# Evicting the up-projection's products ahead of the preceding tile's convolution

## The chip, the cores and the metric

One core of a Trainium2 chip runs the whole program. The metric is device time in microseconds (us) from start to end of one execution, lower is better. The engines that matter are TensorE (PE in the profile; its weight loads are PEld), VectorE (DVE), ScalarE (ACT), GpSimd (POOL) and SyncE (SP, which issues the DMAs).

## The reference, cut to what matters

The model is a trunk of two layers: a token mixer (gated DeltaNet, then mLSTM), each followed by a feed-forward block with a causal convolution of three taps. The change touches the first half of that block, `h @ w_up` and what is done with it:

```python
FFN_DIM = 2816; FFN_CONV = 3; D_MODEL = 1024          # 16 + 1024 tokens

def conv_ffn(h, w_up, conv_w, conv_b, w_down):
    u = causal_depthwise_conv(h @ w_up, conv_w) + conv_b
    gate, up = u[..., :FFN_DIM], u[..., FFN_DIM:]
    return (jax.nn.silu(gate) * up) @ w_down
```

## The kernel before

Features lie on partitions, tokens along the free axis; the 1040 tokens are cut into two halves `t` of 520, and each half into two quarters `n` of 260. The 5632 rows of `w_up` make 22 tiles `j`: 128 gate features (`h = 0`) and the 128 up features that go with them (`h = 1`). Every fp32 product is three matmuls of split operands (`mm3`, L229 to L231): high by high, high by low, low by high.

`ffn_plan` sets the order of the tiles in each layer. Tiles 0 to 5 are first done for half 0 alone, by plain products (`plain`). Then come, six times, a **pair** (tile 6 to 11, both halves) and a **single** (tile 0 to 5, half 1 alone), and then the pairs 12 to 21. Pairs and singles use Strassen's scheme: `quad` makes seven weight combinations from four loaded blocks, and a half needs seven products of four features blocks each, 12 matmuls of 260 columns. So a single has 7 products and a pair 14, the two halves alternating.

`combine` (L193) takes product `i` of a half out of its PSUM bank as soon as it is done. Product 0 is copied by ACT into the temporary `m1` (L199). Every later product is added by DVE (L196) to a temporary, into another temporary or into one of the four results `u`; product 3 takes two such adds. In the rows the names lose their digits: `m_u` is m1, `u_u` is u2 or u3, `u` a result. The products rotate through four PSUM banks (tags `pj` and `sp`, two each, L95 to L101): a product can start when the product four before it has been evicted.

After the last product of a tile its **convolution** follows: for each half, quarter and `h`, ACT scales `u` into a PSUM bank (`z`, L1272), DVE adds the two earlier taps (L1274, whose last step for `h = 1` writes `y`), ACT applies silu (L1276), POOL multiplies gate and up (L1277), and SP stores the result (L1279).

The weights of the tiles ahead are made in between: SP loads a block (L168), DVE forms the combinations (L171, L174, L175, L177: s1, s3, s2, s4), ACT rounds each to its high part (L137, `wh`), POOL subtracts for the low part (L138, `wl`). The combination s2 is written over a11 (L175, after a11's split), and s4 over s2 (L177, after s2's split). There are five slots for split weights, so the split of a weight waits until TensorE is done with the weight five before it.

Each engine works its instructions off in one order. It is set at build time by a scheduler that places an instruction, by priority, in the order of the program; `tc.high_priority(n)` moves what is inside it ahead by `n` of its steps. The accumulations of the down-projection had it before (in `second`); the evictions in `combine` did not. The three temporaries of a half (`temps`, L214) came from the ring `C` of 19 pages, which also holds the results `u` and the products `y`.

Of the kernel before, what the change touches and what calls it, by code (L numbers as in the profile page):

```python
# [29 lines left out]
QB = HB // 2  # L30
# [6 lines left out]
N_PAGES = 19  # L37
# [44 lines left out]
class Trunk:  # L82
# [111 lines left out]
    def combine(self, i, ps, tmp, out):  # L194

        add = lambda o, u: self.nc.vector.tensor_tensor(o, ps[:, :QB], u, ALU.add)  # L196
        m1, u2, u3 = tmp
        if i == 0:
            self.nc.scalar.copy(m1, ps[:, :QB])  # L199
        elif i == 1:  # L200
            add(u2, m1)
        elif i == 2:
            add(u3, u2)
        elif i == 3:
            add(out[3], u3)
            add(u2, u2)
        elif i == 4:
            add(out[1], u2)
        elif i == 5:
            add(out[2], u3)  # L210
        else:
            add(out[0], m1)

    def temps(self, name):  # L214
        return [self.page("C", f"{n}_{name}", N_PAGES)[:, :QB] for n in ("m1", "u2", "u3")]

    def queue_weights(self, sources, ahead):

# [1275 lines left out]
```

## Time and profile before

| | |
|---|---|
| three runs | 3479.31, 3480.08, 3485.89 us (median 3480.08) |
| the profiled execution | 3479.74 us, of which the span from first to last instruction is 3477.9 |
| busy share of the span | PE 92%, PEld 89%, DVE 68%, POOL 48%, ACT 46% |
| up-projection with pairs and singles, layer 1 | about 1458 to 1885 us from the span's start |
| the same, layer 2 | about 2771 to 3200 us |

The profile is of one execution. A row of a timeline gives the start, the duration, the instruction, and in brackets how long its engine was idle just before and what released it. Matmuls overlap in the pipeline: each is shown with some 0.28 us though one starts every 0.12 us, so the spacing of their starts is what counts. A row of busy time by stretch gives the stretch and its length, then the busy time and the number of instructions of PE, PEld, DVE, ACT and POOL, then the granted TensorE clock as a share of full speed, the DMA share and GB/s. A row of waits gives who waited for whom, the total in us, how often, and the longest.

### The profile page before, as it was taken

Reading aid. Unit: us, or ns where it says so; the run is one execution under the profiler, and the core shown is the slowest. Engines: PE = TensorE matmul, PEld = TensorE weight load, DVE = VectorE, ACT = ScalarE, POOL = GpSimd, SP = SyncE. Lnnn points to the kernel's source line nnn. Section 1 sums busy time; section 2 is a strip of 40 time slices with the busy share of each in tenths; the row PEclk is TensorE's granted clock in tenths of the full one; section 3 lists DMA queues with packets and bytes.
Section 4 is the critical chain, followed back from the end, with each engine's and each line's share of the span. In section 5 each row is a group of like instructions: output and inputs, shape, how many; then the busy total and the mean of one; then the engine's idle time right before and its main releaser. Section 6 shows DMA issues by size and latency. Waiting matters only on the chain. (4 is left out here: it accounts for less than half of the span.)

```text
span 3477.9 us, 68427 instructions
## 1 busy us (share of the span) xinstructions
PE 3208.6 (92%) x25368; PEld 3105.4 (89%) x25368; DVE 2368.7 (68%) x5143; ACT 1606.1 (46%) x3390; POOL 1653.5 (48%) x1890
## 2 busy tenths in 40 slices
PE   8999999999998997889999989899998898999998
PEld 6899988988998997888999989899998788999998
DVE  7777787777777559776666484534479766667474
ACT  5455554555545335644544343323355644445232
POOL 2434443443433444576665434323344577665453
PEclk9999999999999999999999999999999899999999
DMA  3010110101101344322223453211134422224452
GB/s 116 25 37 31 34 34 28 34 32 33 34 32 52 105 157 139 122 89 80 85 74 127 146 179 119 84 38 56 55 104 159 145 81 86 74 74 131 133 177 86
DMA packets 234510, 297.73 MB, mean 86 GB/s; under 512 B 20684, under 2 KB 167104, under 8 KB 234176
## 3 DMA queue, kind: packets, MB, share of 16 engines
q1 hardware_dynamic: 234176, 293.37, 26.0%
q8 instruction: 199, 3.26, 0.4%
q14 instruction: 135, 1.11, 0.1%
HBM read 240.06 MB, written 53.23 MB: 84 GB/s over the span
## 5 line engine op out<-in xcount | busy, mean ns | idle before, releaser
L229 PE MATMUL pj_gi<-xh_in,wh_gi 128*128 128x348 f32 x1152 | 393.7, 342 | 5.7 <-ACT wh_gi L137 3.8
L231 PE MATMUL pj_gi<-xh_in,wl_gi 128*128 128x348 f32 x1152 | 395.5, 343 | 0.9 <-POOL wl_gi L138 0.9
L230 PE MATMUL pj_gi<-xl_in,wh_gi 128*128 128x348 f32 x1152 | 392.9, 341 | 0.0
L229 PE MATMUL dn_f<-so_f,wh_f 128*128 128x260 f32 x1344 | 383.5, 285 | 8.1 <-ACT y L1276 3.9
L231 PE MATMUL dn_f<-so_f,wl_f 128*128 128x260 f32 x1344 | 380.5, 283 | 1.9 <-POOL wl_f L138 1.9
L230 PE MATMUL dn_f<-so_f,wh_f 128*128 128x260 f32 x1344 | 380.6, 283 | 0.0
L138 POOL TENSOR_TENSOR wl_f<-wr_f,wh_f 128x512 fp32r<-128x512 f32 x168 | 225.3, 1358 | 243.0 <-PE dn_f L230 102.7
L138 POOL TENSOR_TENSOR wl_u_s<-wr_u,wh_u_s 128x512 fp32r<-128x512 f32 x176 | 228.7, 1303 | 99.6 <-ACT wh_u_s L137 98.6
L1274 DVE SCALAR_TENSOR_TENSOR z<-u,fcw,z 128x260 f32<-128x260 f32 x528 | 244.3, 487 | 42.6 <-ACT z L1272 38.9
L229 PEld LDWEIGHTS dn_f<-so_f,wh_f 128*128 128x128 f32 x1344 | 254.0, 189 | 9.7 <-ACT y L1276 4.3
L437 DVE TENSOR_TENSOR acc_f<-acc_f,dn_f 128x260 f32<-128x260 f32 x320 | 132.7, 420 | 188.7 <-PE dn_f L231 187.6
L231 PEld LDWEIGHTS dn_f<-so_f,wl_f 128*128 128x128 f32 x1344 | 254.2, 189 | 2.4 <-POOL wl_f L138 2.3
L230 PEld LDWEIGHTS dn_f<-so_f,wh_f 128*128 128x128 f32 x1344 | 254.2, 189 | 0.2
L1272 ACT ACTIVATE z<-u,fcb,fcw 128x260 f32<-128x260 f32 x352 | 189.2, 566 | 138.0 <-DVE u L196 136.5
L229 PEld LDWEIGHTS pj_gi<-xh_in,wh_gi 128*128 128x128 f32 x1152 | 221.7, 192 | 8.0 <-ACT wh_gi L137 4.1
L231 PEld LDWEIGHTS pj_gi<-xh_in,wl_gi 128*128 128x128 f32 x1152 | 221.9, 193 | 2.3 <-POOL wl_gi L138 1.1
L230 PEld LDWEIGHTS pj_gi<-xl_in,wh_gi 128*128 128x128 f32 x1152 | 221.7, 192 | 0.7 <-issue 0.2
L138 POOL TENSOR_TENSOR wl_gi<-wr_gi,wh_gi 128x512 fp32r<-128x512 f32 x96 | 132.3, 1379 | 158.6 <-ACT wh_gi L137 152.0
L138 POOL TENSOR_TENSOR wl_u_a<-wr_u,wh_u_a 128x512 fp32r<-128x512 f32 x132 | 171.2, 1297 | 68.1 <-ACT wh_u_a L137 68.0
L693 DVE SCALAR_TENSOR_TENSOR gy<-u_g,c_gdn_conv_w_g,gy 128x348 f32<-128x348 f32 x288 | 188.2, 664 | 7.9 <-ACT gy L691 5.4
L137 ACT CAST wh_u_s<-wr_u 128x512 fp32r<-128x512 f32 x176 | 106.9, 614 | 183.1 <-PE up L230 149.7
L137 ACT CAST wh_f<-wr_f 128x512 fp32r<-128x512 f32 x168 | 103.0, 617 | 173.2 <-PE dn_f L230 119.4
(501 smaller groups left out, 11665.7 us busy)
## 6 DMA issues: line engine op xcount, KB each, us to landing
wr_u<-in_ffn_w_up_dram SPq DMA_DIRECT2D x224, 256.0 KB, 2.7
wr_f<-in_ffn_w_down_dram SPq DMA_DIRECT2D x176, 256.0 KB, 2.8
wr_gi<-in_gdn_w_in_dram SPq DMA_DIRECT2D x96, 256.0 KB, 2.6
h<-y SPq DMA_DIRECT2D x176, 130.0 KB, 2.4
si_f<-h SPq DMA_DIRECT2D x88, 260.0 KB, 3.5
wr_go<-in_gdn_w_out_dram SPq DMA_DIRECT2D x64, 256.0 KB, 2.7
wr_mi<-in_ml_w_in_dram SPq DMA_DIRECT2D x44, 256.0 KB, 2.6
o_g<-gy SPq DMA_DIRECT2D x48, 174.0 KB, 1.8
```

Of the source, the lines that this page charges most:

```text
L137: nc.scalar.copy(hi, part(raw))
L138: nc.gpsimd.tensor_tensor(lo, part(raw), hi.bitcast(F32), ALU.subtract)
L229: nc.tensor.matmul(out, w[0], x[0], start=start, stop=False)
L230: nc.tensor.matmul(out, w[0], x[1], start=False, stop=False)
L231: nc.tensor.matmul(out, w[1], x[0], start=False, stop=stop)
L437: nc.vector.tensor_tensor(acc[m][n], acc[m][n], ps, ALU.add)
L693: ins = nc.vector.scalar_tensor_tensor(y, u[:, j : j + BS], taps[:, j : j + 1], y, ALU.mult, ALU.add)
L1272: nc.scalar.activation(z, p[:, 2 : 2 + QB], AF.Identity, scale=taps[:, 2:3], bias=self.fcb[:, tt : tt + 1])
L1274: nc.vector.scalar_tensor_tensor(z if i or not h else y[h], p[:, i : i + QB], taps[:, i : i + 1], z, ALU.mult, ALU.add)
```

## The change

`combine` wraps its instructions in `high_priority(300)`, and the temporaries come from three other tags of two buffers each: m1 from `part`, u2 from `rs`, u3 from `sum`. Those tags exist already, for norms and sums outside this stretch. The arithmetic is the same.

```diff
--- before.py
+++ after.py
@@ -195,6 +195,10 @@
 
         add = lambda o, u: self.nc.vector.tensor_tensor(o, ps[:, :QB], u, ALU.add)
         m1, u2, u3 = tmp
+        with self.tc.high_priority(300):
+            self.combine_now(i, ps, add, m1, u2, u3, out)
+
+    def combine_now(self, i, ps, add, m1, u2, u3, out):
         if i == 0:
             self.nc.scalar.copy(m1, ps[:, :QB])
         elif i == 1:
@@ -212,7 +216,7 @@
             add(out[0], m1)
 
     def temps(self, name):
-        return [self.page("C", f"{n}_{name}", N_PAGES)[:, :QB] for n in ("m1", "u2", "u3")]
+        return [self.page(tag, f"{n}_{name}", 2)[:, :QB] for n, tag in (("m1", "part"), ("u2", "rs"), ("u3", "sum"))]
 
     def queue_weights(self, sources, ahead):
```

The order of the matmuls is the same but for four of them at the start of the down-projection. On DVE, ACT, POOL and SP the order changes only within the two up-projections. The lines after the new ones carry numbers higher by 4 (L199 is L203, L1272 is L1276, L1274 is L1278, L1276 is L1280).

First place, DVE: the end of pair 9's convolution while single 3's products are running. `u_u` and `u_3_..` are single 3's adds (`up_3_1_i` is its product `i`), `z_9` and `y_9` the convolution, and `wr_u_0_10` the weights of pair 10. Before:

```order
L1274 SCALAR_TENSOR_TENSOR z_9_1_0_1_21581<-u_9_1_0_1_21334,fcw_17463,z_9_1_0_1_21581 128x260
L1274 SCALAR_TENSOR_TENSOR y_9_1_1_0_21572<-u_9_1_1_0_21333,fcw_17463,z_9_1_1_0_21573 128x260
L1274 SCALAR_TENSOR_TENSOR z_9_1_0_1_21581<-u_9_1_0_1_21334,fcw_17463,z_9_1_0_1_21581 128x260
L1274 SCALAR_TENSOR_TENSOR z_9_1_1_1_21588<-u_9_1_1_1_21335,fcw_17463,z_9_1_1_1_21588 128x260
L175 TENSOR_TENSOR wr_u_0_10_0_21594<-wr_u_0_10_4_21598,wr_u_0_10_0_21594 128x512
L1274 SCALAR_TENSOR_TENSOR y_9_1_1_1_21587<-u_9_1_1_1_21335,fcw_17463,z_9_1_1_1_21588 128x260
L196 TENSOR_TENSOR u_u_3_1_21636<-up_3_1_1_21656,m_u_3_1_21635 128x260
L196 TENSOR_TENSOR u_u_3_1_21637<-up_3_1_2_21670,u_u_3_1_21636 128x260
L177 TENSOR_TENSOR wr_u_0_10_0_21594<-wr_u_0_10_3_21597,wr_u_0_10_0_21594 128x512
L196 TENSOR_TENSOR u_3_1_1_1_21641<-up_3_1_3_21684,u_u_3_1_21637 128x260
L196 TENSOR_TENSOR u_u_3_1_21636<-up_3_1_3_21684,u_u_3_1_21636 128x260
L196 TENSOR_TENSOR u_3_1_0_1_21640<-up_3_1_4_21699,u_u_3_1_21636 128x260
```

and with the change, where the add of product 1 stands three rows above the first row shown:

```order
L196 TENSOR_TENSOR u_u_3_1_21637<-up_3_1_2_21670,u_u_3_1_21636 128x260
L1278 SCALAR_TENSOR_TENSOR z_9_1_0_0_21566<-u_9_1_0_0_21332,fcw_17463,z_9_1_0_0_21566 128x260
L1278 SCALAR_TENSOR_TENSOR z_9_1_0_1_21581<-u_9_1_0_1_21334,fcw_17463,z_9_1_0_1_21581 128x260
L1278 SCALAR_TENSOR_TENSOR y_9_1_1_0_21572<-u_9_1_1_0_21333,fcw_17463,z_9_1_1_0_21573 128x260
L1278 SCALAR_TENSOR_TENSOR z_9_1_0_1_21581<-u_9_1_0_1_21334,fcw_17463,z_9_1_0_1_21581 128x260
L1278 SCALAR_TENSOR_TENSOR z_9_1_1_1_21588<-u_9_1_1_1_21335,fcw_17463,z_9_1_1_1_21588 128x260
L175 TENSOR_TENSOR wr_u_0_10_0_21594<-wr_u_0_10_4_21598,wr_u_0_10_0_21594 128x512
L1278 SCALAR_TENSOR_TENSOR y_9_1_1_1_21587<-u_9_1_1_1_21335,fcw_17463,z_9_1_1_1_21588 128x260
L196 TENSOR_TENSOR u_3_1_1_1_21641<-up_3_1_3_21684,u_u_3_1_21637 128x260
L196 TENSOR_TENSOR u_u_3_1_21636<-up_3_1_3_21684,u_u_3_1_21636 128x260
L177 TENSOR_TENSOR wr_u_0_10_0_21594<-wr_u_0_10_3_21597,wr_u_0_10_0_21594 128x512
L196 TENSOR_TENSOR u_3_1_0_1_21640<-up_3_1_4_21699,u_u_3_1_21636 128x260
```

The adds of products 1 and 2 move ahead of eight and six steps of the convolution and of L175, and the two adds of product 3 move ahead of s4 (L177); the adds of products 4, 5 and 6 stay behind L177.

Second place, ACT: the same stretch. `m_u_3` is the copy of single 3's product 0, `wh_u_1_3` the last two weights of single 3, and `wh_u_0_10` the first of pair 10. Before:

```order
L1276 ACTIVATE y_9_0_0_0_21535<-z_9_0_0_0_21536 128x260
L137 CAST wh_u_1_3_a_21314<-wr_u_1_3_2_21283 128x512
L1272 ACTIVATE z_9_1_0_0_21566<-u_9_1_0_0_21332,fcb_17464,fcw_17463 128x260
L1272 ACTIVATE z_9_1_1_0_21573<-u_9_1_1_0_21333,fcb_17464,fcw_17463 128x260
L137 CAST wh_u_1_3_a_21318<-wr_u_1_3_3_21284 128x512
L1276 ACTIVATE y_9_0_0_1_21550<-z_9_0_0_1_21551 128x260
L1272 ACTIVATE z_9_1_0_1_21581<-u_9_1_0_1_21334,fcb_17464,fcw_17463 128x260
L1272 ACTIVATE z_9_1_1_1_21588<-u_9_1_1_1_21335,fcb_17464,fcw_17463 128x260
L1276 ACTIVATE y_9_1_0_0_21565<-z_9_1_0_0_21566 128x260
L137 CAST wh_u_0_10_a_21604<-wr_u_0_10_0_21594 128x512
L1276 ACTIVATE y_9_1_0_1_21580<-z_9_1_0_1_21581 128x260
L199 COPY m_u_3_1_21635<-up_3_1_0_21642 128x260
```

and with the change:

```order
L1280 ACTIVATE y_9_0_0_0_21535<-z_9_0_0_0_21536 128x260
L137 CAST wh_u_1_3_a_21314<-wr_u_1_3_2_21283 128x512
L203 COPY m_u_3_1_21635<-up_3_1_0_21642 128x260
L1276 ACTIVATE z_9_1_0_0_21566<-u_9_1_0_0_21332,fcb_17464,fcw_17463 128x260
L1280 ACTIVATE y_9_0_0_1_21550<-z_9_0_0_1_21551 128x260
L137 CAST wh_u_1_3_a_21318<-wr_u_1_3_3_21284 128x512
L1276 ACTIVATE z_9_1_1_0_21573<-u_9_1_1_0_21333,fcb_17464,fcw_17463 128x260
L1276 ACTIVATE z_9_1_0_1_21581<-u_9_1_0_1_21334,fcb_17464,fcw_17463 128x260
L1276 ACTIVATE z_9_1_1_1_21588<-u_9_1_1_1_21335,fcb_17464,fcw_17463 128x260
L137 CAST wh_u_0_10_a_21604<-wr_u_0_10_0_21594 128x512
L1280 ACTIVATE y_9_1_0_0_21565<-z_9_1_0_0_21566 128x260
L1280 ACTIVATE y_9_1_0_1_21580<-z_9_1_0_1_21581 128x260
```

The copy moves ahead of four scalings, three silus and two casts, and the silu of quarter 1 ahead of a cast.

Third place, ACT in the pairs that follow pairs: the convolution of pair 13 and the copies of pair 14's product 0 (two, one for each half). Before:

```order
L1276 ACTIVATE y_13_0_0_0_23318<-z_13_0_0_0_23319 128x260
L1272 ACTIVATE z_13_1_0_0_23349<-u_13_1_0_0_23115,fcb_17464,fcw_17463 128x260
L1272 ACTIVATE z_13_1_1_0_23356<-u_13_1_1_0_23116,fcb_17464,fcw_17463 128x260
L1276 ACTIVATE y_13_0_0_1_23333<-z_13_0_0_1_23334 128x260
L137 CAST wh_u_0_14_a_23097<-wr_u_0_14_2_23066 128x512
L1272 ACTIVATE z_13_1_0_1_23364<-u_13_1_0_1_23117,fcb_17464,fcw_17463 128x260
L1272 ACTIVATE z_13_1_1_1_23371<-u_13_1_1_1_23118,fcb_17464,fcw_17463 128x260
L1276 ACTIVATE y_13_1_0_0_23348<-z_13_1_0_0_23349 128x260
L1276 ACTIVATE y_13_1_0_1_23363<-z_13_1_0_1_23364 128x260
L137 CAST wh_u_0_14_a_23101<-wr_u_0_14_3_23067 128x512
L199 COPY m_u_14_0_23418<-up_14_0_0_23432 128x260
L199 COPY m_u_14_1_23421<-up_14_1_0_23446 128x260
```

and with the change:

```order
L1280 ACTIVATE y_13_0_0_0_23318<-z_13_0_0_0_23319 128x260
L1276 ACTIVATE z_13_1_0_0_23349<-u_13_1_0_0_23115,fcb_17464,fcw_17463 128x260
L203 COPY m_u_14_0_23418<-up_14_0_0_23432 128x260
L1276 ACTIVATE z_13_1_1_0_23356<-u_13_1_1_0_23116,fcb_17464,fcw_17463 128x260
L1280 ACTIVATE y_13_0_0_1_23333<-z_13_0_0_1_23334 128x260
L203 COPY m_u_14_1_23421<-up_14_1_0_23446 128x260
L137 CAST wh_u_0_14_a_23097<-wr_u_0_14_2_23066 128x512
L1276 ACTIVATE z_13_1_0_1_23364<-u_13_1_0_1_23117,fcb_17464,fcw_17463 128x260
L1280 ACTIVATE y_13_1_0_0_23348<-z_13_1_0_0_23349 128x260
L1276 ACTIVATE z_13_1_1_1_23371<-u_13_1_1_1_23118,fcb_17464,fcw_17463 128x260
L137 CAST wh_u_0_14_a_23101<-wr_u_0_14_3_23067 128x512
L1280 ACTIVATE y_13_1_0_1_23363<-z_13_1_0_1_23364 128x260
```

The copies move from behind the whole convolution to its middle; the last cast moves ahead of the last silu.

## Rows read from the trace of the kernel before

**Rows 1.** Busy time by stretch, the two up-projections
```profile
1458.00:1885.00 427.00, 393.28 (x3198) 386.39 (x3196) 292.14 (x654) 207.21 (x429) 285.41 (x381) 1.00 0.27 90
...
2771.00:3200.00 429.00, 395.14 (x3209) 388.09 (x3209) 294.71 (x659) 208.72 (x432) 286.89 (x383) 1.00 0.27 90
```

**Rows 2.** Waits of PE, 1458 to 1885 us
```profile
PE up L229 <- ACT m_u L199: 19.0, 15, 2.4
PE up L229 <- DVE u_u L196: 14.5, 12, 1.3
```

**Rows 3.** Timeline of PE around a single
```profile
1582.54 0.28 PE L229 MATMUL up<-b_go,wh_u_a 128*128 128x260 f32 x1
...
1589.86 0.39 PE L229 MATMUL up<-b_go,wh_u_s 128*128 128x260 f32 x1 [1.39 <-ACT m_u L199]
...
1597.10 0.39 PE L229 MATMUL up<-b_go,wh_u_a 128*128 128x260 f32 x1 [1.12 <-DVE u_u L196]
```

**Rows 4.** Timeline of PE, pairs that follow pairs
```profile
1716.08 0.40 PE L229 MATMUL up<-t_go,wh_u_s 128*128 128x260 f32 x1 [1.21 <-ACT m_u L199]
...
1716.56 0.28 PE L229 MATMUL up<-t_go,wh_u_s 128*128 128x260 f32 x1
...
1730.56 0.28 PE L229 MATMUL up<-b_go,wh_u_a 128*128 128x260 f32 x1
...
1868.43 0.58 PE L229 MATMUL up<-t_go,wh_u_s 128*128 128x260 f32 x1 [2.38 <-ACT m_u L199]
```

**Rows 5.** Busy time by stretch, one period of each kind in each layer
```profile
1589.86:1624.73 34.87, 31.29 (x252) 30.46 (x253) 24.08 (x53) 16.89 (x35) 25.30 (x33) 1.00 0.27 85
...
1716.08:1737.69 21.61, 20.39 (x168) 20.18 (x168) 14.39 (x35) 10.08 (x22) 13.19 (x20) 1.00 0.23 77
...
2833.91:2868.72 34.81, 31.23 (x252) 30.41 (x252) 24.09 (x53) 16.89 (x35) 25.29 (x33) 1.00 0.26 85
...
3051.32:3072.86 21.54, 20.40 (x168) 20.18 (x168) 14.40 (x35) 10.07 (x22) 13.19 (x20) 1.00 0.22 76
```

**Rows 6.** Timeline of ACT, around the single and in a pair
```profile
1584.73 0.61 ACT L137 CAST wh_u_a<-wr_u 128x512 fp32r<-128x512 f32 x1
...
1585.24 1.07 ACT L1272 ACTIVATE z<-u,fcb,fcw 128x260 f32<-128x260 f32 x2
...
1589.44 0.37 ACT L199 COPY m_u<-up 128x260 f32<-128x260 f32 x1
...
1737.26 0.66 ACT L199 COPY m_u<-up 128x260 f32<-128x260 f32 x2
```

**Rows 7.** Timeline of DVE, around the single and in pairs
```profile
1576.06 0.69 DVE L177 TENSOR_TENSOR wr_u<-wr_u,wr_u 128x512 f32<-128x512 f32 x1 [0.83 <-POOL u L1261]
...
1585.11 0.48 DVE L1274 SCALAR_TENSOR_TENSOR z<-u,fcw,z 128x260 f32<-128x260 f32 x1
...
1588.64 0.88 DVE L1274 SCALAR_TENSOR_TENSOR z<-u,fcw,z 128x260 f32<-128x260 f32 x2
...
1591.37 0.69 DVE L175 TENSOR_TENSOR wr_u<-wr_u,wr_u 128x512 f32<-128x512 f32 x1 [1.85 <-POOL wl_u_a L138]
...
1592.37 0.42 DVE L196 TENSOR_TENSOR u_u<-up,m_u 128x260 f32<-128x260 f32 x1
...
1594.61 1.77 DVE L177 TENSOR_TENSOR wr_u<-wr_u,wr_u 128x512 f32<-128x512 f32 x1 [1.28 <-POOL wl_u_s L138]
...
1717.83 0.43 DVE L196 TENSOR_TENSOR u_u<-up,u_u 128x260 f32<-128x260 f32 x1 [1.00 <-PE up L231]
```

**Rows 8.** Timeline of POOL around the single
```profile
1585.46 1.29 POOL L138 TENSOR_TENSOR wl_u_a<-wr_u,wh_u_a 128x512 fp32r<-128x512 f32 x1
...
1590.04 1.29 POOL L138 TENSOR_TENSOR wl_u_a<-wr_u,wh_u_a 128x512 fp32r<-128x512 f32 x1
...
1592.59 0.74 POOL L1277 TENSOR_TENSOR y<-y,y 128x260 f32<-128x260 f32 x1 [1.25 <-issue]
...
1593.30 2.53 POOL L138 TENSOR_TENSOR wl_u_s<-wr_u,wh_u_s 128x512 fp32r<-128x512 f32 x2
```

## The prediction

> **What bounds the kernel now.** I read the busy time by stretch first. In the two stretches of pairs and singles, TensorE has 393 of 427 us and 395 of 429, at a granted clock of 1.00, the upper level of 2.4 GHz; DVE has 292, POOL 285, ACT 207 [rows 1]. So TensorE sets the pace, and its 34 idle us are what can be had. The waits say for what: 15 times for the copy into m1, 12 times for an add of DVE, 33.5 us in all [rows 2]. The timeline of TensorE gives their pattern, the same in both layers: each of the six singles shows one wait for the copy and two for adds (the copy and the last of them are in [rows 3]), and each of the nine pairs that follow a pair one wait for the copy [rows 4], 6 + 9 = 15 and 2 x 6 = 12.
>
> What a wait costs is more than its idle figure. From 1716.56 to 1730.56 us run 39 groups of three matmuls undisturbed [rows 4], 0.359 each, so a product (four groups) takes 1.436 us, a pair (14) 20.10, a single and a pair (21) 30.16. The periods are 21.61 and 34.87 us in layer 1, 21.54 and 34.81 in layer 2 [rows 5]: 1.5 us lost per pair that follows a pair, 4.7 per single and pair.
>
> Why the evictions are late is on ACT and DVE. The single's first product starts at 1582.54 [rows 3] and is complete by 1584.0; its copy starts at 1589.44 [rows 6], behind the preceding pair's convolution, and the fifth product, which needs that bank, at 1589.86 [rows 3] instead of 1582.54 + 4 x 1.436 = 1588.28. The add of product 1 starts at 1592.37 [rows 7].
>
> **Pairs that follow pairs.** The pair whose copies start at 1737.26 [rows 6] began its products at about 1730.6 (four products and the 1.2 us wait before 1737.7, where its fifth starts, the end of the period in [rows 5]). Product 0 of half 0 is complete at 1732.3. In the new order the first copy stands behind one scaling, the second behind another and a silu: about 1733.2 and 1734.3, each 0.4 us, against needs at 1736.3 and 1737.8. The moved adds then sit among the convolution's steps; DVE is busy 14.4 of 20.1 us, POOL 13.2 [rows 5], and the weight work there follows TensorE's own progress. I count the whole loss as gone: 8 pairs a layer x 2 layers x 1.47 = 23.5 us, 16 at the least if a third of it stays. The ninth wait, 2.38 us idle at 1868.43 [rows 4], costs 2.6; it lies at the handover to the down-projection, where casts of its operands and the last convolution are queued behind. I count half as kept: 1.3 x 2 = 2.6 us (bounds 0 and 5.3).
>
> **Singles and the pair behind them.** Here the wait moves, and I follow the new order step by step through the trace's durations. ACT: the cast at 1584.73 is where the copy now comes next, in place of the scalings at 1585.24 [rows 6], so m1 is there at 1585.6 and the fifth product does not wait. DVE: the step at 1585.11 [rows 7], one more, then the add of product 1 at 1585.95 (product complete at 1585.6), two steps, the add of product 2 at 1587.85 (complete at 1587.1), five steps of about 0.4 each (two take 0.88 at 1588.64 [rows 7]), until 1590.2. Products 5 and 6 do not wait either. Then L175 needs the low part of the next pair's a11. POOL, from its split at 1585.46 in steps of 1.25 us a split and 0.7 a multiplication [rows 8], does: split, two multiplications, split, and the split of a11 from 1589.4 to 1590.6 (1590.04 before). L175 runs to 1591.3, one convolution step to 1591.75, the two adds of product 3 to 1592.5. The next pair's first product could start at 1582.54 + 7 x 1.436 = 1592.6: no wait, barely.
>
> The next pair's second product needs the add of product 4, and that stands behind L177. L177 waits for the low part of s2. POOL's last multiplication follows that convolution step (1591.85), then s2's split runs 1592.55 to 1593.85 (1593.30 before [rows 8]). L177 took 1.77 us when POOL's next split ran beside it, and 0.69 when not [rows 7]; POOL's next split follows at once again, so I take 1.77. That ends at 1595.65, the add at 1596.0, and the product starts there rather than at 1582.54 + 8 x 1.436 = 1594.03: 2.0 us, with the restart 2.15 lost, in one wait in place of three. The period becomes 30.16 + 2.15 = 32.3, a gain of 2.55; 12 singles give 30.6 us. Through the pair the delayed convolution catches up: the split of the single after next waits for TensorE anyway.
>
> The Trainium skill, "SBUF — State Buffer", section "SBUF: two separate sides", says that a DVE operation with two SBUF inputs and a GpSimd operation that reads SBUF lock each other out, the first one for its whole instruction. The two durations of L177 agree with it. If the lock missed, each single would gain 1.08 us more, 13 us in all, and the time would be 3410 us.
>
> Bounds of this term: each step of the chain can move by about one us, the price seen between the two L177s, so 1.45 to 3.65 a single, 17 to 44 us.
>
> **Edits without a price.** The new pages: a half's m1 is read last by the add of product 6, and its buffer is wanted again two halves later, in pairs some 2 us after that add, so the copy need not wait. Ring `C` loses six claims per pair and only gets looser; no wait for it is in the rows. On SP one weight load per single steps behind a store; that load is for a tile a pair later, some 20 us of cover. If it were late, L177 would be, at 12 us for each us.
>
> **The sum.** 23.5 + 2.6 + 30.6 = 56.7 us. The profiled execution took 3479.74, so 3423.0; the median of the runs is 0.3 above it: 3423.4, say 3423. Bounds of the terms: 16 + 0 + 17 = 33 and 23.5 + 5.3 + 44 = 73, so 3407 to 3447.
>
> **Rivals.**
> 1. Every wait goes, in the singles too: 12 x 4.7 = 56.4, 23.5 and 5.3: 3395. For it: DVE has 24.1 busy us in 30.2 [rows 5]. Against it: L177 stays ahead of the adds of products 4 to 6 in the order. Chance 0.08.
> 2. The moved adds hold DVE. An add that reaches the head of DVE's order before its product is complete stops the convolution behind it, and through POOL L175 and L177. Waits of this kind are in the trace, 1.00 us at 1717.83 [rows 7]. In my walk the adds come 0.35 and 0.75 us after their products; if both came too early at the full price, L177 ends 2 us later, a single gains 0.55, and the sum is 6.6 + 26.1 = 33: 3447. Without any gain in the singles it is 3454. Chance 0.12. The Trainium skill, "PSUM — Partial Sum Buffer", section "Engine vs sequencer instructions", calls the queues of ScalarE, VectorE and GpSimd strict FIFO; it is the rule that speaks against moving evictions up.
> 3. Slower than before: the last silu chain. The silu of quarter 1 now stands behind the copy and a scaling on ACT. If it ends after 1587.4, POOL's second multiplication is late, with the splits of the single's last weight, a11 and s2 behind it, then L177, then the bank. Each us beyond it costs 12 us. My walk has that silu end at 1586.4, one us ahead; the singles' gain is gone at 2.55 us of lateness, the kernel is slower from 4.7 us, and at 6 us it takes 3495. Nothing in the rows is that long. Chance 0.06.
> 4. It doesn't do what it says: the copies move, but each waits at the head of ACT's order for its page's last reader, so that all starts as before: 3480. The margin of 2 us above speaks against it. Chance 0.06.
>
> **Numbers.** My forecast has 0.68, with 3407 to 3447. Rival 2 lies above it; together they hold 0.80, so the range is 3403 to 3455. A measurement of this kernel can tell about 0.2%, 7 us, from no change. Faster: 0.68 + 0.08 + 0.12 = 0.88; within 0.2%: 0.06; slower: 0.06.
>
> **What would show it.** In the changed profile, TensorE's waits for m_u fall from 15 a layer to about none, its waits for adds from 12 to about 6 of 1.5 to 2 us, each before the second product of a pair behind a single; pairs repeat every 20.1 to 20.2 us, single and pair every 32.3; DVE's L177 still shows 1.7 us in the singles. The prediction is wrong if waits for the low weight parts (POOL, L138) appear on TensorE, or if DVE's waits for TensorE at the moved adds are long.

## The result and the profile after

The changed kernel takes 3443.86 us (median of four runs, 3441.42 to 3455.35) where the kernel before takes 3482.98 in the same comparison: a ratio of 0.990, 95% interval 0.9883 to 0.9917. The profiled execution is 3444.23 us, its span 3442.5, 35.4 less than before. The forecast was 3423, so the direction and the range held, and some 21 us of the forecast gain are missing.

Where the 35 us come from shows when both profiles are cut at the same instructions (starts of the first matmul, read from the timelines of TensorE; times and differences each rounded):

| stretch | before | after | difference |
|---|---|---|---|
| start to the first product of the pairs, layer 1 | 1457.8 | 1460.9 | +3.2 |
| pairs and singles, layer 1 | 426.6 | 404.7 | -21.9 |
| down-projection, layer 1 | 271.4 | 276.2 | +4.8 |
| from there to the pairs of layer 2 | 615.9 | 613.4 | -2.5 |
| pairs and singles, layer 2 | 426.3 | 407.5 | -18.8 |
| down-projection, layer 2, to its last matmul | 263.7 | 264.1 | +0.4 |
| the rest | 16.2 | 15.6 | -0.6 |

The two stages of the change give 40.7 us; the rest takes 5.3 back. The +3.2 ahead of the change is in stretches where both kernels run the same order. A run with the order of before, below, shows 3.7 there, and over the fourteen profiles of this document that stretch takes 1455.7 to 1466.8 us, so I count it as the difference between two executions.

Busy time by stretch for those two stages (columns as in [rows 1]):

```profile
1461.00:1865.60 404.60, 391.72 (x3193) 389.18 (x3192) 290.18 (x650) 206.28 (x425) 282.83 (x378) 0.98 0.28 92
2755.20:3162.80 407.60, 395.01 (x3195) 392.55 (x3194) 292.07 (x651) 206.40 (x425) 283.67 (x377) 0.97 0.28 91
```

TensorE is idle for 13 us in each stage where it was idle for 34 [rows 1], but the granted clock, 1.00 in both stages before, is now 0.98 and 0.97. TensorE's waits over the whole run answer [rows 2]:

```profile
PE up L233 <- DVE u L196: 21.5, 12, 1.8
...
PE up L233 <- DVE u_u L196: 1.4, 8, 0.2
```

No wait for m_u is left of 15 a layer. Twelve waits for an add are left, one behind each single, 1.8 us each, and eight of up to 0.2 us. The timeline of TensorE shows one of them, before the second product of the pair that follows a single:

```profile
1594.49 0.39 PE L233 MATMUL up<-b_go,wh_u_a 128*128 128x260 f32 x1 [1.80 <-DVE u L196]
...
1595.68 0.35 PE L233 MATMUL up<-b_go,wh_u_a 128*128 128x260 f32 x1
1595.83 0.42 PE L234 MATMUL up<-b_go,wh_u_a 128*128 128x260 f32 x1
1596.05 0.42 PE L235 MATMUL up<-b_go,wl_u_a 128*128 128x260 f32 x1
1596.27 0.42 PE L233 MATMUL up<-t_go,wh_u_s 128*128 128x260 f32 x1
```

Read the starts: after the idle, matmuls first start 0.12 us apart, and from 1595.83 on 0.22 apart, for sixteen in a row. That is the clock. Busy time by stretch, for periods of single and pair from one such wait to the next, for the sixteen slow matmuls alone (1595.83 to 1599.25), and for 20 us of pairs:

```profile
1494.92:1527.61 32.69, 30.72 (x252) 30.34 (x252) 24.11 (x54) 16.93 (x36) 25.18 (x33) 1.00 0.27 90
1527.61:1560.28 32.67, 30.71 (x253) 30.32 (x253) 24.10 (x54) 16.94 (x36) 25.16 (x33) 1.00 0.27 90
1560.28:1594.49 34.21, 32.24 (x253) 31.85 (x253) 24.25 (x54) 17.04 (x36) 25.20 (x33) 0.95 0.26 86
1595.83:1599.25 3.42, 3.42 (x18) 3.42 (x17) 2.65 (x8) 2.90 (x8) 2.91 (x5) 0.51 0.46 150
1700.00:1720.10 20.10, 20.10 (x170) 20.10 (x169) 14.24 (x35) 10.17 (x21) 13.23 (x19) 1.00 0.25 80
```

The first two periods take 32.7 us at a clock of 1.00. From the third on they take 34.2 at 0.95: behind the same wait the clock falls to its lower level, 1.2 GHz (0.51 over the slow stretch), for 3.4 us. Behind ten of the twelve singles that happens, at 1.5 us each. The pairs run without any wait. Behind the wait is what the prediction said, L177 in its slow form, on DVE:

```profile
1588.58 1.22 DVE L175 TENSOR_TENSOR wr_u<-wr_u,wr_u 128x512 f32<-128x512 f32 x1 [0.50 <-POOL wl_u_a L138]
...
1592.36 1.74 DVE L177 TENSOR_TENSOR wr_u<-wr_u,wr_u 128x512 f32<-128x512 f32 x1 [1.49 <-POOL wl_u_s L138]
1594.02 0.75 DVE L196 TENSOR_TENSOR u<-up,u_u 128x260 f32<-128x260 f32 x2
```

L177 waits 1.49 us for GpSimd's split of s2, runs 1.74, and only then come the adds of products 4 and 5. At the handover to the down-projection, the timeline of TensorE has three waits in layer 1:

```profile
1865.64 0.36 PE L233 MATMUL dn_f<-so_f,wh_f 128*128 128x260 f32 x1 [1.18 <-DVE u L196]
...
1868.54 0.36 PE L233 MATMUL dn_f<-so_f,wh_f 128*128 128x260 f32 x1 [1.94 <-ACT wh_f L137]
...
1873.11 0.59 PE L233 MATMUL dn_f<-so_f,wh_f 128*128 128x260 f32 x1 [1.87 <-ACT y L1280]
```

Before, the one at [rows 4] (2.38) was followed by two, of 0.72 and 1.96 us.

### The profile page after: what moved, and what is told of

Read it like the earlier page. It is cut to its first block, busy times and chain, and to the rows that moved or that the text cites. A ratio compares the mean times of both kernels' runs of the same rounds, so it can differ in the third digit from the quotient of the medians.

```text
span 3442.5 us, 68429 instructions
## 1 busy us (share of the span) xinstructions
PE 3212.2 (93%) x25368; PEld 3119.6 (91%) x25368; DVE 2373.1 (69%) x5143; ACT 1609.0 (47%) x3390; POOL 1652.2 (48%) x1890
## 5 line engine op out<-in xcount | busy, mean ns | idle before, releaser
L1278 DVE SCALAR_TENSOR_TENSOR z<-u,fcw,z 128x260 f32<-128x260 f32 x528 | 243.4, 487 | 49.8 <-ACT z L1276 35.0
L233 PEld LDWEIGHTS dn_f<-so_f,wh_f 128*128 128x128 f32 x1344 | 257.7, 192 | 13.6 <-ACT z L1276 5.5
L234 PEld LDWEIGHTS dn_f<-so_f,wh_f 128*128 128x128 f32 x1344 | 258.2, 192 | 0.2
L1276 ACT ACTIVATE z<-u,fcb,fcw 128x260 f32<-128x260 f32 x352 | 192.3, 570 | 93.7 <-DVE u L196 92.4
```

Of the source, the lines that this page charges most:

```text
L233: nc.tensor.matmul(out, w[0], x[0], start=start, stop=False)
L234: nc.tensor.matmul(out, w[0], x[1], start=False, stop=False)
L1276: nc.scalar.activation(z, p[:, 2 : 2 + QB], AF.Identity, scale=taps[:, 2:3], bias=self.fcb[:, tt : tt + 1])
L1278: nc.vector.scalar_tensor_tensor(z if i or not h else y[h], p[:, i : i + QB], taps[:, i : i + 1], z, ALU.mult, ALU.add)
```

## The experiments

The theory to be tested: the missing gain is the clock's fall behind the wait that is left, and the gain that did come is split between the pages and the priority in some way. Twelve kernels were run. Times on the chip differ a little from one comparison to the next (the kernel before took 3484 to 3491 us beside them), so the ratio to it is what compares; beside it stands the length of the two stages of pairs and singles together, from one profile each, which is sharper: the changed kernel, adds_first and last_plain, which keep the same waits in the stages, lie between 811.9 and 813.2. "Falls" counts, of the twelve places behind the singles, those where TensorE's matmuls went on at 0.22 us.

| kernel | median us | before beside it | ratio (95% interval) | stages, us | falls |
|---|---|---|---|---|---|
| before | 3482.98 | | | 852.9 | 0 |
| changed | 3443.86 | 3482.98 | 0.990 (0.9883 to 0.9917) | 812.2 | 10 |
| prio_only | 3484.82 | 3486.11 | 1.0007 (0.999 to 1.0024) | 852.9 | 0 |
| pages_only | 3464.58 | 3486.11 | 0.9934 (0.9912 to 0.9955) | 823.5 | 3 |
| m1_own | 3461.01 | 3488.32 | 0.9921 (0.9904 to 0.9937) | 826.5 | 8 |
| copy_first | 3457.44 | 3491.09 | 0.990 (0.9869 to 0.9931) | 823.7 | 5 |
| adds_first | 3448.36 | 3491.09 | 0.9878 (0.9845 to 0.9912) | 813.2 | 10 |
| last_plain | 3445.17 | 3491.09 | 0.9868 (0.9839 to 0.9897) | 811.9 | 10 |
| fill4 | 3435.24 | 3486.11 | 0.9855 (0.9834 to 0.9876) | 796.6 | 0 |
| fill1 | 3430.52 | 3484.22 | 0.985 (0.9833 to 0.9867) | 796.3 | 0 |
| s4_pool | 3428.26 | 3486.11 | 0.9832 (0.9815 to 0.9849) | 793.9 | 0 |
| slots_s4 | 3437.03 | 3484.22 | 0.986 (0.9839 to 0.988) | 793.1 | 0 |
| own_s2 | 3437.45 | 3491.09 | 0.9856 (0.9812 to 0.99) | 792.6 | 1 |
| slots_s24 | 3466.55 | 3484.22 | 0.9951 (0.9931 to 0.9971) | 831.8 | 12 |

### Which part of the change does what

**Priority alone** (prio_only).

```diff
-        return [self.page(tag, f"{n}_{name}", 2)[:, :QB] for n, tag in (("m1", "part"), ("u2", "rs"), ("u3", "sum"))]
+        return [self.page("C", f"{n}_{name}", N_PAGES)[:, :QB] for n in ("m1", "u2", "u3")]
```

> Priority alone: the temporaries m1, u2, u3 stay on the large ring C, the evictions still carry the raised priority. In this build the order of DVE's instructions is that of the kernel before, and ACT's differs from it in two places. Theory (the pages are what lets the scheduler move the evictions): as the kernel before, 3480 us, within 4; TensorE waits for m_u about 30 times in all, and for adds 24 times. Rival (the priority does the work): as the changed kernel, 3444 us.

Measured: no change, ratio 1.0007. TensorE's waits in it are those of the kernel before over the whole run:

```profile
PE up L233 <- ACT m_u L203: 37.5, 30, 2.4
PE up L233 <- DVE u_u L196: 28.9, 24, 1.3
```

The order of TensorE, DVE and GpSimd in its trace is that of the kernel before. So the raised priority by itself gains nothing. What kept the evictions late was not their rank in the order of the program.

**Pages alone** (pages_only).

```diff
-        with self.tc.high_priority(300):
-            self.combine_now(i, ps, add, m1, u2, u3, out)
+        self.combine_now(i, ps, add, m1, u2, u3, out)
```

> Pages alone: the temporaries on the other pages, without the raised priority. In this build the copies and adds of the singles have moved up, those of the pairs have not. Theory (the two parts share the gain by stage): the singles gain, the sixteen pairs that follow pairs keep their wait of 1.2 us each (1.47 lost), so 3444 + 23.5 = 3467 us, between 3460 and 3473; TensorE's waits for m_u are about 18, all in pairs. Rival (pages do nothing by themselves): 3480. Rival (pages do everything): 3444.

Measured: 0.9934. On the scale of the first comparison (3483 before) that is 3460 us, at the edge of the theory's range, and the theory's reason is wrong. TensorE has no wait for m_u at all, in the pairs either; all that is left are two waits for adds at each single (before its last product and before the next pair's first):

```profile
PE up L232 <- DVE u_u L196: 43.6, 24, 2.3
```

The expectation had also misread the build: the copies of the pairs have moved. In ACT's timeline the second copy of a pair now stands between the last scaling and the last silu, and the first some 3 us ahead of it:

```profile
1740.30 0.57 ACT L1275 ACTIVATE z<-u,fcb,fcw 128x260 f32<-128x260 f32 x1
1740.79 0.38 ACT L202 COPY m_u<-up 128x260 f32<-128x260 f32 x1
1741.52 0.39 ACT L1279 ACTIVATE y<-z 128x260 f32<-128x260 f32 x1 [0.34 <-DVE z L1277]
```

The stages are 29.4 us shorter than before, of the change's 40.7. So the pages carry the pairs, the copies of the singles and the ninth wait; what they lack against the changed kernel lies in the singles.

**m1's page alone** (m1_own): u2 and u3 back on ring C, priority kept.

```diff
-        return [self.page(tag, f"{n}_{name}", 2)[:, :QB] for n, tag in (("m1", "part"), ("u2", "rs"), ("u3", "sum"))]
+        return [self.page(tag, f"{n}_{name}", k)[:, :QB] for n, tag, k in (("m1", "part", 2), ("u2", "C", N_PAGES), ("u3", "C", N_PAGES))]
```

> The changed kernel with only m1 on another page: u2 and u3 go back to ring C, which then has 20 claims a pair on 19 pages. (In a build the other way round, m1 alone back on ring C, the order of DVE is that of the kernel before, row for row.) Theory (what holds the copy back is the page that m1 claims in ring C): no wait for m_u on TensorE, pairs that follow pairs repeat every 20.1 us, and only the adds of the singles may stand later than in the changed kernel: 3444 to 3460 us. Rival (the ring is too short for all its claims, and any temporary left in it holds the rest): the waits of the pairs stay, 3467 to 3480.

Measured: 0.9921, or 3455 us on that scale, as the theory has it; the same 20 us of pairs as above run without a wait:

```profile
1700.00:1720.10 20.10, 20.10 (x170) 20.10 (x170) 14.32 (x34) 10.18 (x22) 13.23 (x20) 1.00 0.25 78
```

The page that the copy writes is what held it. The adds of the singles, with u2 and u3 back in the ring, are late: a wait of 2.7 to 3.0 us for one is left at each of the twelve. Why a page of the ring holds its writer back is not shown. One could argue from the count: a pair claimed 22 pages of ring C (six temporaries, eight results, eight products of the convolution) and the ring has 19, so a claim falls on a page that an earlier tile's work still holds, and the scheduler places the writer behind that work. But the build named in the expectation, with m1 alone back on the ring, claims 18 pages a pair and has DVE's order of before all the same, so the count is not the whole reason. What the traces show is that the order itself changes with the page, and that no wait tells of it.

**The copy's priority or the adds'** (copy_first, shown, and adds_first, which has `i > 0` there).

```diff
-        with self.tc.high_priority(300):
-            self.combine_now(i, ps, add, m1, u2, u3, out)
+        if i == 0:
+            with self.tc.high_priority(300):
+                self.combine_now(i, ps, add, m1, u2, u3, out)
+        else:
+            self.combine_now(i, ps, add, m1, u2, u3, out)
```

> The changed kernel with the raised priority for ACT's copy of product 0 alone; DVE's adds keep their usual priority, the pages are the changed ones. Theory (a pair that follows a pair waits only for the copy, that frees its bank): the sixteen waits for m_u are gone and those pairs repeat every 20.1 us; the singles stay as with the pages alone (single and pair 34.5 us in place of 34.2): 3444 + 12 x 0.3 = 3448 us, from 3443 to 3453. Rival (the pairs need the adds moved too): a wait for an add in each pair, 1.47 x 16 more, about 3467.

> The changed kernel with the raised priority for DVE's adds alone; ACT's copy keeps its usual priority. Theory: the first add needs the copy, so moving the adds without it gains nothing in the pairs: sixteen waits for m_u of 1.2 us stay, 3444 + 23.5 = 3467 us, and more if adds at the head of DVE's order hold the convolution. Rival (the adds carry the gain): 3444.

Measured: 0.990 and 0.9878. The intervals overlap, the stages don't: 823.7 us for copy_first, as with the pages alone, and 813.2 for adds_first, as in the changed kernel. TensorE's waits, of copy_first and then of adds_first:

```profile
PE up L236 <- DVE u_u L196: 42.2, 24, 2.5
```

```profile
PE up L236 <- DVE u L196: 21.6, 12, 1.8
```

With the copy's priority alone two waits for adds stay at each single; with the adds' alone it is the one wait of 1.8 us. For copy_first the pairs and the singles came out as expected. For adds_first the theory fails: the copies need no priority once they have their own page.

**The handover** (last_plain).

```diff
-                self.combine(i, ps, tmp[t], [u[t, h, n][:, 2 : 2 + QB] for h in range(2) for n in range(2)])
+                self.combine(i, ps, tmp[t], j < NF - 1, [u[t, h, n][:, 2 : 2 + QB] for h in range(2) for n in range(2)])
...
-        with self.tc.high_priority(300):
+        with self.tc.high_priority(300 if early else 0):
```

> The changed kernel without the raised priority in the last pair of each layer, the one before the down-projection. Theory (the handover gives back what its ninth wait gained): the wait of 2.4 us for m_u in the last pair returns, the waits for wh_f and for the add before the first products of the down-projection shrink to 0.7 in all, and the time is that of the changed kernel, 3444 us, within 3. Rival (half of the ninth wait's gain is kept, as predicted): 2.6 us longer, 3447; the first product of the down-projection's steady part is then later by 1.3 us a layer.

Measured: 0.9868, stages of 811.9 us, and no wait for m_u: the last pair's copy, too, was freed by its page, so this run doesn't undo the handover. It tells nothing on how much of the ninth wait's gain is kept.

### What the wait that is left costs

**Work in place of idle time** (fill4; fill1 is the same with `range(1)`, one group of three matmuls in place of four).

```diff
+                if i == t == 0 and len(halves) == 2 and N_FIRST < j <= 2 * N_FIRST:
+                    for k in range(4):
+                        self.mm3(ps[:, :QB], [z[:, k] for z in w[i]], self.xo[t](i, k), k == 0, k == 3)
                 for k in range(4):
                     self.mm3(ps[:, :QB], [z[:, k] for z in w[i]], self.xo[t](i, k), k == 0, k == 3)
```

> The changed kernel, with the first product of each pair behind a single (12 in all) computed twice into the same bank, so that TensorE has 1.436 us of work in place of most of the 1.80 us idle before the second product: 17.2 us of added matmuls. Theory (the idle of 1.80 us is what lets the granted clock fall, about 1.5 us lost at ten of the twelve places): the idle falls to 0.4 us, the clock stays at 1.00 in all twelve, single and pair repeat every 32.7 us, and the kernel with more work is faster: 3444 - 15 = 3429 us. Rival 1 (the clock falls there for another reason): 3444. Rival 2 (the wait follows TensorE's own progress, so added work adds): 3461.

> As the run with the product computed twice, but only its first group of three matmuls is repeated (0.36 us): the idle before the second product shrinks from 1.80 to 1.44 us, a little more than the waits of 1.1 to 1.4 us of the kernel before, behind which the clock stayed at 1.00. Theory A (the length of the idle decides, and 1.44 is on the side of the kernel before): no fall at the twelve places, 32.7 us for single and pair, 3444 - 15 = 3429 us. Theory B (the 2.5 us gaps that left the clock alone in the other kernels show that length alone doesn't decide): falls at some of the twelve places, 3432 to 3444 us.

Measured: fill4 0.9855, fill1 0.985; both are faster than the changed kernel though they do more. Their intervals lie below its own, but overlap those of adds_first and last_plain, which keep its waits; the stages tell them apart. The waits of fill4, and a period of it:

```profile
PE up L233 <- DVE u L196: 4.6, 12, 0.4
```

```profile
1531.81:1564.48 32.67, 32.17 (x265) 31.78 (x265) 24.62 (x54) 16.98 (x36) 25.25 (x33) 1.00 0.31 91
```

A period takes 32.67 us with twelve more matmuls in it, exactly what the changed kernel takes where its clock stays up, and the clock is 1.00 behind all twelve waits. The stages are 15.6 us shorter than the changed kernel's: the ten falls, at 1.5 each. In fill1 the wait is still there:

```profile
1555.08 0.39 PE L233 MATMUL up<-b_go,wh_u_a 128*128 128x260 f32 x1 [1.47 <-DVE u L196]
```

1.47 us idle in place of 1.80, no fall in twelve, 15.9 us shorter. So 0.36 us of useless work in each wait has the whole effect. Theory A holds for this length.

### Taking the wait away

**s4 on GpSimd** (s4_pool).

```diff
-        v.tensor_tensor(s4, a12, s2, ALU.subtract)
+        self.nc.gpsimd.tensor_tensor(s4, a12, s2, ALU.subtract)
```

> The changed kernel, with the subtraction that makes s4 (L177) on GpSimd in place of DVE, behind the split of s2 that it has to wait for, so that no add stands behind that wait. Theory (L177's wait for POOL is what holds the add of product 4, and with it the second product of the pair): all twelve waits of 1.80 us and the clock's falls behind them go, 12 x 1.96 + 10 x 1.5 = 38.5 us: 3405 us, from 3398 to 3415. Rival (GpSimd, 21 subtractions a layer longer, is late with the low parts of the weights): waits for wl_u on TensorE, 3430 to 3460.

Measured: 0.9832 (0.9815 to 0.9849), 18.3 us less in the stages than the changed kernel, and the lowest ratio of all (several other intervals overlap its own). The wait before the pair's second product is gone at all twelve places, so L177 on DVE was its cause. But most of the gain has another reason than the theory's. In place of that wait others came, before the pair's first product (1.3 to 1.6 us, at ten places) and before its fourth (0.5 us, at twelve); TensorE's waits:

```profile
PE up L233 <- DVE u_u L196: 11.2, 8, 1.6
...
PE up L233 <- DVE u L196: 5.9, 12, 0.5
...
PE up L233 <- ACT wh_u_s L137: 2.7, 2, 1.4
```

Together 19.8 us, hardly less than the 22.9 for up in the changed kernel, and a period is 32.6 us (one is 32.8). But no single one is longer than 1.6 us, and the clock never fell: ten falls at 1.5 us are 15 of the 18.3. The timeline of DVE shows what is behind the new waits:

```profile
1554.79 1.22 DVE L175 TENSOR_TENSOR wr_u<-wr_u,wr_u 128x512 f32<-128x512 f32 x1 [0.50 <-POOL wl_u_a L138]
...
1556.33 0.42 DVE L196 TENSOR_TENSOR u<-up,u_u 128x260 f32<-128x260 f32 x1
...
1561.20 0.69 DVE L171 TENSOR_TENSOR wr_u<-wr_u,wr_u 128x512 f32<-128x512 f32 x1 [3.26 <-POOL wl_u_s L138]
1561.81 0.42 DVE L196 TENSOR_TENSOR u<-up,m_u 128x260 f32<-128x260 f32 x1
```

The adds of product 3 now stand behind L175, and the add of product 6 behind L171, each of which waits for GpSimd. I tried to take these away too.

**Other slots** (slots_s4 and slots_s24: both have s4 on GpSimd as above and the first two lines below, and slots_s24 has the last two as well).

```diff
-        a11, a21, a22, a12, s1 = [self.raw_slot(f"{name}_{i}") for i in range(5)]
+        a21, s1, a22, a11, a12 = [self.raw_slot(f"{name}_{i}") for i in range(5)]
...
-        v.tensor_tensor(s2, s1, a11, ALU.subtract)
+        self.nc.gpsimd.tensor_tensor(s2, s1, a11, ALU.subtract)
```

> The kernel with s4 made on GpSimd, and the five raw slots of a tile claimed in another order (a21, s1, a22, a11, a12 in place of a11, a21, a22, a12, s1), so that the slot of the next tile's s1 was last used by a part that is split early. Theory (L171 waits 3.3 us for GpSimd because its slot is the one of s4, and holds the add of product 6): the twelve waits of 0.5 us before the pair's fourth product go, 12 x 0.65 = 8 us less than 3428: 3420 us; the ten waits of 1.35 us behind L175 stay. Rival (DVE's order is built anew and something else is late): 3425 to 3435.

> The same claims of slots, and both in-place subtractions, s2 and s4, on GpSimd; DVE makes only s1 and s3, which wait for no split of the same tile. Theory (every remaining wait in the singles comes from DVE's in-place subtractions): no wait over 0.3 us in the twelve singles and their pairs, 30.2 to 30.6 us for single and pair: 3428 - 8 - 12 x 1.5 = 3402 us. Rival (GpSimd, two subtractions of 1.29 us a tile longer, is late with the low parts): waits for wl_u or for casts on TensorE, 3420 to 3450.

Measured: 0.986 and 0.9951. Both theories fail. In slots_s4 the stages stay at 793.1 us with the same waits of 0.5 us. In slots_s24 one wait of 3.3 us behind each single, before the pair's fourth product, is all that is left, and it is worse:

```profile
PE up L233 <- DVE u L196: 39.6, 12, 3.4
```

```profile
1597.61 0.69 DVE L171 TENSOR_TENSOR wr_u<-wr_u,wr_u 128x512 f32<-128x512 f32 x1 [5.15 <-POOL wl_u_s L138]
1598.34 1.78 DVE L174 TENSOR_TENSOR wr_u<-wr_u,wr_u 128x512 f32<-128x512 f32 x1
1600.04 0.42 DVE L196 TENSOR_TENSOR u<-up,m_u 128x260 f32<-128x260 f32 x1
```

L171 stands 5.15 us for GpSimd at the head of DVE, with an add behind it. The clock fell behind all twelve.

**A slot for s2** (own_s2).

```diff
-        s3, s2, s4 = a21, a11, a11
+        s3, s2, s4 = a21, self.raw_slot(f"{name}_5"), a11
...
-N_RAW, N_SPLIT = 9, 10
+N_RAW, N_SPLIT = 10, 10
...
-N_PAGES = 19
+N_PAGES = 18
```

> The changed kernel with s2 in a slot of its own (six raw slots a tile in a ring of ten in place of five in a ring of nine; ring C has 18 pages in place of 19), so that neither L175 nor L177 overwrites what GpSimd still has to split. Theory (both in-place subtractions hold adds behind a wait for GpSimd): the waits before the pair's second product go in all twelve places without a new one in the single, 1.96 x 12 + 1.5 x 10 = 38.5 us less than 3444: 3405 us, from 3400 to 3415. Rival (the wait for GpSimd moves to the slots' reuse, at L171 or L175 in the pairs): waits for adds in pairs, 3425 to 3450.

Measured: 0.9856, some 3433 us on the scale of the first comparison, so the forecast time was missed. In the stages the theory holds in part: 19.6 us less than the changed kernel, and periods down to 31.3 us. The waits before the pair's second product are gone, but in their place waits of 0.6 to 3.4 us stand before its first, at all twelve places. Another 12.7 us are lost elsewhere, between the down-projection of layer 1 and the up-projection of layer 2 (519.7 us against 507.0), with waits of TensorE there that the changed kernel doesn't have:

```profile
PE pj_mi L233 <- DVE my L308: 7.2, 12, 1.0
...
PE fs_omo L302 <- DVE ss_omo L295: 2.3, 1, 2.3
```

`my` is a page of ring C in the mLSTM, and that ring has one page less here; whether that or the longer ring of raw slots is the cause was not separated.

## Why the prediction was right or wrong

**What bounds the kernel: right.** TensorE's waits of [rows 2] were what was to be had, and the stages gave 40.7 of the 68 us of idle time in [rows 1].

**Pairs, 23.5 us: right in size and in the order walked, wrong on what makes that order.** The waits are gone and a pair takes 20.10 us (the row of 1700 to 1720.10). The prediction read the new order of ACT rightly, but put the pages under "Edits without a price" and wrote that ring `C` "only gets looser; no wait for it is in the rows". That is the step that failed: without the pages the order of DVE and the time stay (prio_only, 1.0007), and with m1's page alone the pairs that follow pairs lose their wait (m1_own). Of rival 4 (it does not do what it says) the priority alone is the case, though not by a wait at the head of ACT.

**The ninth wait, 2.6 us: not kept.** In the stage itself more came than its price: TensorE ran slowly behind it before, too, which the trace of before shows and the prediction did not read (busy time by stretch, kernel before):

```profile
1868.43:1871.82 3.39, 3.39 (x15) 3.39 (x16) 3.01 (x7) 1.24 (x3) 2.58 (x2) 0.50 0.55 164
```

Gap and fall together were 2.55 + 1.6 = 4.1 us a layer, 8.3 in all. The handover takes as much back. From the last matmul of the pairs to the 200th of the down-projection (busy time by stretch; first the two layers of the kernel before, then of the changed kernel):

```profile
1884.26:1911.56 27.30, 24.62 (x202) 24.17 (x201) 17.72 (x41) 11.09 (x21) 13.37 (x27) 1.00 0.38 124
3197.86:3225.14 27.28, 24.64 (x203) 24.18 (x202) 17.73 (x41) 11.09 (x21) 12.96 (x15) 1.00 0.39 123
```

```profile
1864.18:1897.50 33.32, 28.33 (x202) 27.67 (x201) 21.27 (x49) 13.83 (x27) 16.03 (x31) 0.85 0.43 139
3161.61:3192.19 30.58, 25.92 (x202) 25.26 (x201) 21.03 (x49) 13.69 (x26) 16.16 (x19) 0.94 0.47 153
```

That is 6.0 and 3.3 us longer, 9.3 in all: 2.3 and 2.0 of idle time (the waits of layer 1 above and their like in layer 2), the rest the same matmuls at a clock of 0.85 and 0.94 in place of 1.00. The other kernels with changed pages take 30.5 to 33.7 us for this stretch, and prio_only, with the order of before, 28.7 and 28.6, so this is no chance. The step "I count half as kept" failed: of what the ninth wait gave, nothing is left at this point. Behind it layer 2 takes 1.9 us less than before and layer 1 as long. Over the whole down-projection the loss is so 1.3 and 1.0 us before the first matmul, +4.8 in layer 1 and +0.4 in layer 2. That leaves about 1 us net over both layers, with one execution on each side; that it lies within the bounds of 0 to 5.3 is luck.

**Singles, 30.6 us: the chain was right, the price of its wait was not.** The place (second product of the pair), the cause (L177 behind GpSimd's split, and 1.74 us long), the count (12) and the length (2.0 forecast, 1.80 idle and 2.08 between starts measured) came as walked. The period was to be 32.3. It is 32.68 where the clock stays up: 0.4 more, since "no wait, barely" before the pair's first product became a wait of some 0.2 us idle, 0.4 lost with the restart. Behind that is L175, which the walk had at 0.7 us and which ran 1.22 in the singles (the row at 1588.58). And it is 34.2 at ten of twelve places, because the step "with the restart 2.15 lost" counted the wait at its length, and the clock's fall behind it costs another 1.5. So the term is 12 x 2.16 - 10 x 1.5 = 11 us in place of 30.6, below its lower bound of 17, and 15 of the 20 us that are missing in it are the clock, which fill4 and fill1 gave back. The time stayed above the range's slow end because the pairs gave all of their 23.5, where the lower bound had 16.

**The sum by these terms**, for the two stages: 23.5 for pairs, 8.3 - 2.3 at the handover, 11 for singles, 40.5 against 40.7 measured. Outside them 5.3 us are lost by the table at the start, 4.8 of them in the down-projection of layer 1.

**Rivals.** The time is 3 us from rival 2's (3447), but its mechanism is not there: DVE's waits for TensorE at the adds of u_u fell, between 1461 and 1866 us from 31.2 us to 19.2. The silu chain of rival 3 did not come: in the two stages TensorE has no wait for a low part. The Trainium skill, "SBUF — State Buffer", section "SBUF: two separate sides", states the lock that the prediction drew on. The trace agrees with it: L177 takes 1.74 us beside GpSimd's split and 0.69 in the pairs, and L175 takes 1.22 us where a multiplication of GpSimd has started just before it and 0.69 in the pairs.

## What to carry to other kernels

A buffer from a shared ring can hold an instruction back without any wait in the trace, because the order was already built around it: when a raised priority moves nothing, look at what the instruction writes to. Price a wait of a saturated TensorE by the starts of the matmuls behind it, in the trace at hand, and not by its idle figure alone; the trace of before had the case, behind the last of [rows 4]. And follow a wait that you take away to the end of the next stage: the ninth one's gain was gone 200 matmuls later. Where a wait can't be removed, making it shorter, or splitting it in two, can be worth as much: here 0.36 us of repeated matmuls in it gained 1.3 us each time.

## What was not expected of the hardware

TensorE's clock fell behind waits far shorter than the stages around them: 1.80 us idle after more than 30 us of dense matmuls brought 3.4 us at 0.51 of the clock. By the length of the idle, at the places behind the singles: up to 1.6 us never (before, prio_only, fill1, fill4, s4_pool, slots_s4); 1.80 us at ten of twelve (changed, adds_first and last_plain, each); 2.0 us at neither of two (own_s2); about 2.25 us at three of twelve (pages_only) and five (copy_first); about 2.8 us at eight (m1_own); 3.3 us at twelve of twelve (slots_s24) and 3.4 at its one place (own_s2). At the handover 2.4 us did it in both layers of before and of prio_only. So a longer idle does not always do more, and the length alone does not decide in between. In the changed kernel the same wait left the clock up twice and let it fall four times in layer 1, and once it had fallen it fell in every period that followed in that layer; in last_plain it fell at the second and third place of layer 1, not at the fourth, and again at the fifth and sixth. What picks the places stays open; no run here was made to tell.

The Trainium skill, "TensorE: Matmul & The Clock Gate", section "HAM oscillation — how this bites in real kernels", describes a kernel whose clock falls again at every step of a loop because of the wait between steps. At ten of the twelve places of the changed kernel the clock falls so, behind a wait for an add. The idle gaps that the section lets pass are longer than the 1.80 us that were enough here, so for that the measurement decides.
